# The input norm's vector: eight rows transposed once, and multiplied in at the transposed x

## The chip, the cores and the metric

The kernel runs on one core of a Trainium2 chip. The metric is the device time of one execution in microseconds (us); lower is better. Five engines run side by side, each through its own list of instructions in order: PE (TensorE, the matmuls; its weight loads are listed apart as PEld), DVE (VectorE), ACT (ScalarE), POOL (GpSimd) and SP (SyncE, which here issues DMAs). They wait for each other by semaphores.

## The reference, cut to what matters

One decoder layer on 512 tokens of width 1024, all in float32. It begins with a norm, whose result feeds every projection of the first half:

```python
def rms_norm(x, g):
    xf = x.astype(jnp.float32)
    y = xf * lax.rsqrt(jnp.mean(xf * xf, axis=-1, keepdims=True) + EPS)
    return (y * g.astype(jnp.float32)).astype(x.dtype)

u = rms_norm(x, norm_mix_g[l])
proj = u @ w_in[l]          # q, k, v, the convolution's input, two gates
```

After it come sliding-window attention, a convolution, a gated sum with `w_out`, and an MLP with a second norm. The change touches only the first norm, `u`, and the order of the work around it.

## The kernel before, in words

**Precision.** Every float32 matrix is split into a high part (rounded to the matmul's float32r) and a low part (what is left), and a product is three matmuls: high by high, low by high and high by low. So each operand costs a high copy (ACT, usually) and a low subtraction (DVE or POOL).

**The stretch that the change touches.** The first 38 us make `u` transposed, with channels on partitions (`uTh` and `uTl`, high and low), and from it k and v for all tokens. The 512 tokens are four tiles (t = 0 to 3) of 128. For each tile:

- `x_square(t)`: ACT squares x with a running sum (L296) and takes a root (L297); DVE makes the reciprocal root with a Newton step (L150, L127 to L130).
- `x_scale(t)`: one DVE instruction over 128x1024 multiplies x by the root (one number per partition, that is per token) and by `gmix` (L300). `gmix` is the norm's vector copied to all 128 partitions, since here the channels lie along the free dimension; it comes by a DMA of 128 copies of 4 KB, 512 KB.
- `x_trans(t)`, that is `transpose_split`: for each half of the channels four PE transposes (L207) fill one bank of PSUM, `tp`, a 128x512 tile. Then one ACT copy of 128x512 makes the high part (L209), and one DVE subtraction of 128x512 the low part (L210).
- `k_proj(t)` and `v_proj(t)`, by `tok_proj`: 16 matmuls of 256 columns in eight pairs, for each 128 channels first the high part of u (L316) then the low one (L317) by the weights' high part; then eight by the weights' low part (L320).

The weights of k come in two halves of 512 KB into `kw_raw` (L235), those of v into `vw_raw`. ACT casts each half to its high part (L307); the low parts (L308) are made by POOL for k's first half and by DVE for the other three.

**What sets the order.** From L1341 on this stretch stands in an order written out by hand under `manual_schedule`: each of PE, DVE, ACT and POOL gets its instructions in the order of the calls, and an instruction that waits holds back what stands behind it on its engine. DMAs are issued by SP in program order: x's first tile, `gmix`, the two halves of k's weights, x's second tile, the halves of v's weights, x's last two tiles, then small vectors. Before its first real work PE runs `WARM` = 20 dummy matmuls of the 128x128 identity by itself (`warm_up`, two instructions each, L225), and `FILL` = 4 more between the first tile's transposes and its k. After this stretch the rest (events sorted by position) follows: columns of small vectors (L361), then the projections from L498 on.

Buffers of the `pt` tag are three tiles of 128x1024: `gmix` takes one, and the `u_t` tiles the others in turn. The tiles in PSUM with the tag `tr` are two, so the two halves of a `tp` are two banks.

Of the kernel before, what the change touches and what calls it, by code (L numbers as in the profile page):

```python
# [8 lines left out]
F32 = mybir.dt.float32  # L9
F32R = mybir.dt.float32r  # L10
I32 = mybir.dt.int32
AF = mybir.ActivationFunctionType
# [5 lines left out]
P = 128  # L18
S = 512
# [21 lines left out]
WARM = 20  # L41
FILL = 4
# [11 lines left out]
def tile_hybrid_block(  # L54
# [44 lines left out]
    def bc(ap, n):  # L99
        return ap.partition_broadcast(n)  # L100
# [47 lines left out]
    def mean_eps(ss, n, w, tag):  # L148
        ms = sm.tile([P, w], F32, name=f"ms_{tag}", tag=f"ms{w}")
        ve.tensor_scalar(out=ms, in0=ss, scalar1=1.0 / n, scalar2=EPS, op0=ALU.mult, op1=ALU.add)  # L150
        return ms
# [49 lines left out]
    def transpose_split(ps_pool, src, dst_h, dst_l, t, tag, pt="tr"):  # L201

        for half in range(2):
            tp = ps_pool.tile([P, 4, P], F32, name=f"tp_{tag}_{half}", tag=pt)
            for j in range(4):
                k = half * 4 + j
                pe.transpose(tp[:, j, :], src[half][:, j * P:(j + 1) * P], ident)  # L207
            hs = dst_h[:, half * 4:half * 4 + 4, t * P:(t + 1) * P]
            se.copy(hs, tp)  # L209
            ve.tensor_tensor(out=dst_l[:, half * 4:half * 4 + 4, t * P:(t + 1) * P],  # L210
                             in0=tp, in1=hs.bitcast(F32), op=ALU.subtract)
# [27 lines left out]
    gmix = att.tile([P, D], F32, name="gmix", tag="pt", bufs=3)  # L239
    kw_raw = wp.tile([P, KD, 256], F32, name="raw_k", tag="raw", bufs=2)  # L240
    nc.sync.dma_start(gmix, bc(norm_mix_g[0], P))
# [14 lines left out]
    nsink = rb_sink[:, 32:32 + NQ]  # L256
    nc.sync.dma_start(gq, bc(q_norm_g[0], P))
# [41 lines left out]
    def x_scale(t, rs):  # L299
        ve.scalar_tensor_tensor(out=us[t], in0=xt[t], scalar=rs, in1=gmix, op0=ALU.mult, op1=ALU.mult)  # L300

    def x_trans(t):
        transpose_split(ps1, (us[t][:, 0:S], us[t][:, S:D]), uTh, uTl, t, f"u{t}")
# [1037 lines left out]
    with tc.manual_schedule(engines=START_ENGINES):  # L1341
        se.activation(roots[:, 0:1], epsc, AF.Sqrt)
        x_square(0, ss0)
        x_scale(0, rsqrt_root(root[0], mean_eps(ss0, D, 1, "x0"), 1, "x0"))
        lo0 = hi_lo(kw, kw_raw, 0, se.copy, ge)
        lo0()
        load(0)
        x_trans(0)
        warm_up(FILL)
        lo1 = hi_lo(kw, kw_raw, 1, se.copy, ve)  # L1350
        lo1()
# [12 lines left out]
        x_square(3, ss2[:, 1:2])  # L1364
        next(vp)
        rs2 = rsqrt_root(roots[:, 2:4], mean_eps(ss2, D, 2, "x23"), 2, "x23")
        ksum()
        next(vp)
        x_scale(2, rs2[:, 0:1])
# [3 lines left out]
        x_trans(2)  # L1373
        split_hi(0)
# [3 lines left out]
        for _ in vp:  # L1378
            pass
# [54 lines left out]
```

## Time and profile before

| what | value |
|---|---|
| median of 3 runs | 772.23 us (771.13 to 772.3) |
| the profiled execution | 770.88 us, of which its span is 769.1 us |
| PE busy | 759.5 us (99%) |
| DVE busy | 603.8 us (79%) |
| ACT busy | 440.3 us (57%) |
| POOL busy | 275.2 us (36%) |

The span runs from the first instruction to the end of the last; times in the rows below count from its start. "Busy" is the time in which an engine had an instruction under way. A matmul's record is longer than the interval at which matmuls follow each other, because they are pipelined. A row of the timeline gives start, duration, engine, line of the kernel, operation, output and inputs, sizes (partitions x elements) and count; in square brackets stands the idle time before it and what ended it.

### The profile page before, as it was taken

What the parts mean: (1) busy time and instruction counts of PE and PEld (TensorE: products, weight loads), DVE (VectorE), ACT (ScalarE), POOL (GpSimd) and SP (SyncE); (2) the same over time, 40 slices, a digit from 0 to 9 for tenths busy, and PEclk for the clock granted to TensorE, in tenths of its full rate; (3) what the DMA queues carried; (4) which work ended last, traced back from release to release, by engine and by line L of the source; (5) the groups of instructions that cost most, each with busy time, mean ns of one, the idle gap of its engine ahead of it and who ended that gap; (6) DMA issues with size and microseconds to landing.
All of it is one profiled execution on the core that took longest, in us unless ns stands there. A gap on an engine that the chain in (4) does not pass through costs nothing.

```text
span 769.1 us, 11643 instructions
## 1 busy us (share of the span) xinstructions
PE 759.5 (99%) x4476; PEld 667.8 (87%) x4476; DVE 603.8 (79%) x925; ACT 440.3 (57%) x697; POOL 275.2 (36%) x215
## 2 busy tenths in 40 slices
PE   9999999999999999999999999989999999999997
PEld 8989989897888888888888899868998899889986
DVE  5467978898888888877337678899779987998696
ACT  7445457667667656257325367754675467636761
POOL 1454978958575465524440002210121011101110
PEclk9999999999999999999999999999999999999999
DMA  7441051214132122523318107883588348844772
GB/s 267 151 144 55 1 165 41 98 55 136 56 98 96 55 75 90 192 82 109 105 63 312 69 29 151 205 196 105 145 211 186 116 133 216 178 132 115 167 159 109
DMA packets 65870, 97.48 MB, mean 127 GB/s; under 512 B 3524, under 2 KB 36340, under 8 KB 65814
## 3 DMA queue, kind: packets, MB, share of 16 engines
q1 hardware_dynamic: 56566, 78.91, 31.1%
q0 software_dynamic: 9248, 17.83, 13.7%
q8 instruction: 35, 0.57, 0.3%
q14 instruction: 21, 0.17, 0.1%
HBM read 94.60 MB, written 2.12 MB: 126 GB/s over the span
## 4 chain that ended last, share of the span: by engine, by line
PE 82%; DVE 6%; ACT 3%; DMA 3%; issue 3%; POOL 2%; DVEq 0%; POOLq 0%; ACTq 0%
PE ps_x L1160 9%; PE ps_z L1165 8%; PE ps_y L1160 4%; PE ps_y L1165 4%; DMA block<-in_w_ff_dram 3%; PE ps_x L1165 3%; PE ps_z L1160 2%; PE ps_ta L498 2%; PE ps_ta L500 2%; PE ps_wo L199 2%; PE ps_wo L198 2%; PE ps_wo L197 2%; PE ps_g L498 2%; PE ps_ta L499 2%; PE ps_wc L500 2%
## 5 line engine op out<-in xcount | busy, mean ns | idle before, releaser
L1135 DVE TENSOR_TENSOR piecel<-block,pieceh 128x1024 fp32r<-128x1024 f32 x112 | 136.1, 1222 | 36.2 <-ACT pieceh L1132 36.0
L1132 ACT CAST pieceh<-block 128x1024 fp32r<-128x1024 f32 x112 | 115.9, 1050 | 73.5 <-DVE block L1129 21.4
L1115 POOL DMA_DIRECT2D block<-in_w_ff_dram x34 | 41.3, 1243 | 298.5 <-DVE piecel L1135 174.6
L800 DVE SCALAR_TENSOR_TENSOR cv<-h,wcol,cv 128x512 f32<-128x512 f32 x208 | 147.7, 749 | 0.5
L1160 PE MATMUL ps_x<-xSh,pieceh 128*128 128x256 f32 x192 | 53.9, 281 | 0.4 <-ACT c L1179 0.4
L1160 PE MATMUL ps_x<-xSl,pieceh 128*128 128x256 f32 x192 | 53.9, 281 | 0.0
L1160 PE MATMUL ps_x<-xSh,piecel 128*128 128x256 f32 x192 | 53.8, 280 | 0.0
L709 ACT ACTIVATE s<-s,negm 128x257 f32<-128x257 f32 (+1 forms) x64 | 30.5, 480 | 16.4 <-DVE negm L701 16.4
L1165 PE MATMUL ps_z<-piecel,aSh 128*128 128x512 f32 x96 | 37.9, 395 | 1.7 <-DVE piecel L1135 1.6
L1165 PE MATMUL ps_z<-pieceh,aSh 128*128 128x512 f32 x96 | 37.5, 390 | 0.5 <-ACT pieceh L1132 0.5
L1165 PE MATMUL ps_z<-pieceh,aSl 128*128 128x512 f32 x96 | 37.4, 389 | 0.0
L733 DVE TENSOR_TENSOR pTl<-ptp,pTh 128x512 fp32r<-128x512 f32 x28 | 19.4, 691 | 22.9 <-ACT pTh L729 22.9
L1129 DVE TENSOR_TENSOR block<-block,block 128x1024 f32<-128x1024 f32 x30 | 36.6, 1223 | 0.7 <-DMA block<-in_w_ff_dram 0.3
L1160 PEld LDWEIGHTS ps_x<-xSh,piecel 128*128 128x128 f32 x192 | 36.7, 191 | 0.0
L197 PE MATMUL ps_q<-wh_q,uTh 128*128 128x256 f32 x128 | 36.6, 286 | 0.0
L1160 PEld LDWEIGHTS ps_x<-xSh,pieceh 128*128 128x128 f32 x192 | 36.0, 188 | 0.6 <-ACT c L1179 0.6
L1160 PEld LDWEIGHTS ps_x<-xSl,pieceh 128*128 128x128 f32 x192 | 36.0, 188 | 0.2 <-DVE xSl L1203 0.2
L199 PE MATMUL ps_q<-wh_q,uTl 128*128 128x256 f32 x128 | 36.2, 283 | 0.0
L198 PE MATMUL ps_q<-wl_q,uTh 128*128 128x256 f32 x128 | 36.2, 283 | 0.0
L792 POOL TENSOR_TENSOR side<-side,tap 128x512 f32<-128x512 f32 x24 | 31.1, 1297 | 13.6 <-ACT tap L791 13.6
L1199 ACT CAST aSh<-c 128x1024 fp32r<-128x1024 f32 x16 | 16.8, 1050 | 28.8 <-DVE c L1213 13.2
L718 POOL TENSOR_TENSOR s<-s,r 128x1024 f32<-128x1024 f32 (+1 forms) x16 | 26.9, 1684 | 14.7 <-DVE r L713 14.7
(323 smaller groups left out, 2540.9 us busy)
## 6 DMA issues: line engine op xcount, KB each, us to landing
block<-in_w_ff_dram SPq DMA_DIRECT2D x64, 512.0 KB, 5.0
block<-in_w_ff_dram POOLq DMA_DIRECT2D x34, 512.0 KB, 6.8
x<-in_x_dram SPq DMA_DIRECT2D x8, 512.0 KB, 5.1
raw_g<-in_w_in_dram SPq DMA_DIRECT2D x8, 512.0 KB, 4.5
raw_a<-in_w_in_dram SPq DMA_DIRECT2D x8, 512.0 KB, 3.6
raw_q<-in_w_in_dram SPq DMA_DIRECT2D x8, 512.0 KB, 4.9
raw_ta<-in_w_in_dram SPq DMA_DIRECT2D x8, 512.0 KB, 4.4
raw_tc<-in_w_in_dram SPq DMA_DIRECT2D x8, 512.0 KB, 3.5
```

The source lines that it names most:

```text
L197: pe.matmul(ps, ah, wh, start=first, stop=False)
L198: pe.matmul(ps, ah, wl, start=False, stop=False)
L199: pe.matmul(ps, al, wh, start=False, stop=last)
L498: pe.matmul(ps, wh[:, k, :], ah(k), start=(k == 0), stop=False)
L792: ge.tensor_tensor(out=side[ct], in0=side[ct], in1=tap, op=ALU.add)
L800: ve.scalar_tensor_tensor(out=cps[ct], in0=src, scalar=w, in1=cps[ct], op0=ALU.mult, op1=ALU.add)
L1115: ge.dma_start(tl["raw"][buf][:, ks, :], block(ph, i, j)[:, ks, :], accum_op=ALU.add)
L1129: ve.tensor_tensor(out=o, in0=a, in1=b, op=ALU.add)
L1132: se.copy(tl["ph"][n % 4], tl["raw"][buf][:, 2 * h:2 * h + 2, :])
L1135: ve.tensor_tensor(out=tl["pl"][n % 4], in0=tl["raw"][buf][:, 2 * h:2 * h + 2, :], in1=tl["ph"][n % 4].bitcast(F32), op=ALU.subtract)
L1160: pe.matmul(o, b[:, c, w], a[:, k, :], start=(first and c + q + i == 0), stop=(k == 3 and i == 2), skip_group_check=True)
L1165: pe.matmul(acc, a[:, k, w], b[:, c, :], start=(first and c + i == 0), stop=(k == 3 and i == 2), skip_group_check=True)
```

## The change

The vector comes as eight rows of 128 numbers (`grow`, a DMA of 4 KB) instead of 128 copies of it. One PE transpose into PSUM (`g_ps`) and one DVE copy make of it eight columns, `gcol`: channel on partition, one column for each 128 channels. `x_scale` multiplies by the root alone. `transpose_split` multiplies by the column where it reads the transposed x: for each half, four ACT activations of 128x128 with the column as scale make the high parts, then four DVE instructions of 128x128 (multiply by the column, subtract the high part) the low ones. Where one ACT and one DVE instruction stood there are four of each, for every half of every tile: 32 and 32 in place of 8 and 8.

The written order changes too. `WARM` goes from 20 to 12, `FILL` from 4 to 1, and two dummy matmuls (`WARM2`) come behind the vector's transpose. ACT's cast of the second half of k's weights moves from behind the first tile's transposes to between their two halves. The square of tile 3 and the reciprocal root of tiles 2 and 3 move behind the rest of v for tile 0. The rest of v for tile 1 moves ahead of the next weights' split and of `x_scale(3)`.

```diff
--- before.py
+++ after.py
@@ -38,8 +38,9 @@
 UNIT0 = 42
 END = 152
 RATES = ((16, 1.0), (42, 1.9), (152, 1.35), (1e9, 1.8))
-WARM = 20
-FILL = 4
+WARM = 12
+WARM2 = 2
+FILL = 1
 EARLY = 3
 ENG = mybir.EngineType
 START_ENGINES = {ENG.PE, ENG.DVE, ENG.Activation, ENG.Pool}
@@ -198,17 +199,22 @@
         pe.matmul(ps, ah, wl, start=False, stop=False)
         pe.matmul(ps, al, wh, start=False, stop=last)
 
-    def transpose_split(ps_pool, src, dst_h, dst_l, t, tag, pt="tr"):
+    def transpose_split(ps_pool, src, dst_h, dst_l, t, tag, weight, between, pt="tr"):
 
         for half in range(2):
             tp = ps_pool.tile([P, 4, P], F32, name=f"tp_{tag}_{half}", tag=pt)
             for j in range(4):
                 k = half * 4 + j
                 pe.transpose(tp[:, j, :], src[half][:, j * P:(j + 1) * P], ident)
-            hs = dst_h[:, half * 4:half * 4 + 4, t * P:(t + 1) * P]
-            se.copy(hs, tp)
-            ve.tensor_tensor(out=dst_l[:, half * 4:half * 4 + 4, t * P:(t + 1) * P],
-                             in0=tp, in1=hs.bitcast(F32), op=ALU.subtract)
+            parts = [(tp[:, j, :], weight[:, half * 4 + j:half * 4 + j + 1],
+                      *(d[:, half * 4 + j, t * P:(t + 1) * P] for d in (dst_h, dst_l))) for j in range(4)]
+            for part, w, hs, ls in parts:
+                se.activation(hs, part, AF.Identity, scale=w)
+            for part, w, hs, ls in parts:
+                ve.scalar_tensor_tensor(out=ls, in0=part, scalar=w, in1=hs.bitcast(F32),
+                                        op0=ALU.mult, op1=ALU.subtract)
+            if half == 0:
+                between()
 
     gp = ExitStack()
     gpool = gp.enter_context(tc.tile_pool(name="gpool", bufs=1))
@@ -236,9 +242,9 @@
                           w_in[512 * kh:512 * kh + 512, c0:c0 + 256].rearrange("(k p) c -> p k c", p=P))
 
     xt = [load_x(0)]
-    gmix = att.tile([P, D], F32, name="gmix", tag="pt", bufs=3)
+    grow = att.tile([P, D], F32, name="grow", tag="pt", bufs=3)[0:KD, 0:P]
     kw_raw = wp.tile([P, KD, 256], F32, name="raw_k", tag="raw", bufs=2)
-    nc.sync.dma_start(gmix, bc(norm_mix_g[0], P))
+    nc.sync.dma_start(grow, norm_mix_g[0].rearrange("(k p) -> k p", p=P))
     load_kv(kw_raw, Q_END, 0)
     load_kv(kw_raw, Q_END, 1)
     xt.append(load_x(1))
@@ -254,6 +260,7 @@
     gq = keep.tile([P, HD], F32, name="gq")
     gk = keep.tile([P, HD], F32, name="gk")
     nsink = rb_sink[:, 32:32 + NQ]
+    gcol = rb_sink[:, 48:48 + KD]
     nc.sync.dma_start(gq, bc(q_norm_g[0], P))
     nc.sync.dma_start(gk, bc(k_norm_g[0], P))
     nc.sync.dma_start(nsink, bc(attn_sinks[0], P))
@@ -297,10 +304,10 @@
         se.activation(root[t], ss, AF.Sqrt, scale=1.0 / D, bias=epsc)
 
     def x_scale(t, rs):
-        ve.scalar_tensor_tensor(out=us[t], in0=xt[t], scalar=rs, in1=gmix, op0=ALU.mult, op1=ALU.mult)
-
-    def x_trans(t):
-        transpose_split(ps1, (us[t][:, 0:S], us[t][:, S:D]), uTh, uTl, t, f"u{t}")
+        ve.tensor_scalar(out=us[t], in0=xt[t], scalar1=rs, scalar2=None, op0=ALU.mult)
+
+    def x_trans(t, between=lambda: None):
+        transpose_split(ps1, (us[t][:, 0:S], us[t][:, S:D]), uTh, uTl, t, f"u{t}", gcol, between)
 
     def hi_lo(dst, raw, j, hi_fn, lo_eng):
         ks = slice(4 * j, 4 * j + 4)
@@ -1341,14 +1348,19 @@
     with tc.manual_schedule(engines=START_ENGINES):
         se.activation(roots[:, 0:1], epsc, AF.Sqrt)
         x_square(0, ss0)
-        x_scale(0, rsqrt_root(root[0], mean_eps(ss0, D, 1, "x0"), 1, "x0"))
+        rs0 = rsqrt_root(root[0], mean_eps(ss0, D, 1, "x0"), 1, "x0")
+        g_ps = ps1.tile([P, KD], F32, name="g_ps", tag="tr")
+        pe.transpose(g_ps, grow, ident[0:KD, 0:KD])
+        ve.tensor_copy(gcol, g_ps)
+        warm_up(WARM2)
+        x_scale(0, rs0)
         lo0 = hi_lo(kw, kw_raw, 0, se.copy, ge)
         lo0()
+        lo1 = []
         load(0)
-        x_trans(0)
+        x_trans(0, lambda: lo1.append(hi_lo(kw, kw_raw, 1, se.copy, ve)))
         warm_up(FILL)
-        lo1 = hi_lo(kw, kw_raw, 1, se.copy, ve)
-        lo1()
+        lo1[0]()
         x_square(1, ss1)
         vlo0 = hi_lo(vw, vw_raw, 0, se.copy, ve)
         vlo1 = hi_lo(vw, vw_raw, 1, se.copy, ve)
@@ -1361,22 +1373,22 @@
         vp = v_proj(0)
         next(vp)
         x_trans(1)
-        x_square(3, ss2[:, 1:2])
         next(vp)
-        rs2 = rsqrt_root(roots[:, 2:4], mean_eps(ss2, D, 2, "x23"), 2, "x23")
         ksum()
         next(vp)
+        x_square(3, ss2[:, 1:2])
+        rs2 = rsqrt_root(roots[:, 2:4], mean_eps(ss2, D, 2, "x23"), 2, "x23")
         x_scale(2, rs2[:, 0:1])
         ksum = k_proj(1)
         vp = v_proj(1)
         next(vp)
         x_trans(2)
+        for _ in vp:
+            pass
         split_hi(0)
         split_lo(0)
         x_scale(3, rs2[:, 1:2])
         ksum()
-        for _ in vp:
-            pass
         split_hi(1)
         split_lo(1)
         ksum = k_proj(2)
```

## Rows read from the trace of the kernel before

**Rows 1.** The page, part 1: busy time, share, instructions of each engine.
```profile
PE 759.5 (99%) x4476; PEld 667.8 (87%) x4476; DVE 603.8 (79%) x925; ACT 440.3 (57%) x697; POOL 275.2 (36%) x215
```

**Rows 2.** The chain of waits, in order of time: start, us, what.
```profile
1.47 7.14 PE warm L225 x40
8.61 0.87 PE tp_u L207 x8
...
12.51 0.96 PE ps_k L320 x8
```

**Rows 3.** Timeline of ACT, from 4 us and at 23 us.
```profile
4.13 1.06 ACT L296 ACTIVATE u<-x 128x1024 f32<-128x1024 f32 x1 [1.89 <-DMA x<-in_x_dram]
...
7.84 1.05 ACT L307 CAST kw<-raw_k 128x1024 fp32r<-128x1024 f32 x1 [2.23 <-DMA raw_k<-in_w_in_dram]
9.09 1.07 ACT L209 CAST uTh<-tp_u 128x512 fp32r<-128x512 f32 x2 [0.20 <-PE tp_u L207]
10.05 1.06 ACT L307 CAST kw<-raw_k 128x1024 fp32r<-128x1024 f32 x1
11.00 1.06 ACT L296 ACTIVATE u<-x 128x1024 f32<-128x1024 f32 x1
...
12.39 2.14 ACT L307 CAST vw<-raw_v 128x1024 fp32r<-128x1024 f32 x2
...
23.12 1.08 ACT L209 CAST uTh<-tp_u 128x512 fp32r<-128x512 f32 x2 [1.69 <-PE tp_u L207]
```

**Rows 4.** Timeline of PE and its weight loads, at 13.5, 24.3 and 38 us.
```profile
13.47 0.19 PEld L316 LDWEIGHTS ps_v<-vw,uTh 128*128 128x128 f32 x1 [0.21 <-ACT vw L307]
...
24.30 0.28 PE L316 MATMUL ps_k<-kw,uTh 128*128 128x256 f32 x1
24.48 0.39 PE L317 MATMUL ps_k<-kw,uTl 128*128 128x256 f32 x1
...
38.01 0.50 PE L498 MATMUL ps_g<-uTh,wh_g 128*128 128x512 f32 x1
```

**Rows 5.** Timeline of DVE, 6 to 12 us.
```profile
6.22 0.16 DVE L130 SCALAR_TENSOR_TENSOR roots<-a_x,roots 128x1 f32<-128x1 f32 x1
6.58 1.29 DVE L300 SCALAR_TENSOR_TENSOR u<-x,roots,gmix 128x1024 f32<-128x1024 f32 x1 [0.20 <-DMA gmix<-in_norm_mix_g_dram]
9.71 1.29 DVE L210 TENSOR_TENSOR uTl<-tp_u,uTh 128x512 fp32r<-128x512 f32 x2 [1.84 <-ACT uTh L209]
11.14 1.30 DVE L308 TENSOR_TENSOR kw<-raw_k,kw 128x1024 fp32r<-128x1024 f32 x1
```

**Rows 6.** The dummy matmuls alone, in two stretches: busy (count), granted clock, DMA.
```profile
2.00:6.00 4.00, 4.00 (x21) 4.00 (x20) 1.00 0.90 263
7.00:8.00 1.00, 1.00 (x11) 1.00 (x10) 1.00 1.08 377
```

**Rows 7.** Timeline of ACT, 107 to 112.2 us: instructions with a column as operand.
```profile
107.72 0.39 ACT L709 ACTIVATE s<-s,negm 128x129 f32<-128x129 f32 x1
108.01 0.19 ACT L709 ACTIVATION_READ_ACCUMULATOR s<-s,negm 128x1 f32 x1
...
111.60 0.69 ACT L811 ACTIVATE h<-cv,wcol 128x512 f32<-128x512 f32 x1 [1.64 <-DVE csum L808]
112.19 1.04 ACT L462 CAST wh_g<-raw_g 128x1024 fp32r<-128x1024 f32 x1
```

**Rows 8.** Timeline of DVE: four taps at 65.67 us, a fill at 38 us.
```profile
65.67 2.73 DVE L800 SCALAR_TENSOR_TENSOR cv<-h,wcol,cv 128x512 f32<-128x512 f32 x4
...
38.04 0.38 DVE L364 MEMSET rel<- 16x384 f32 x1
```

**Rows 9.** Timeline, 115.5 to 117 us: four matmuls into one bank and its reader.
```profile
115.70 0.28 PE L694 MATMUL sp<-kTl,qT 128*128 128x256 f32 x1
...
115.94 0.28 PE L694 MATMUL sp<-kTl,qT 128*128 128x256 f32 x1
...
116.26 0.48 DVE L701 CUSTOM_DVE_ANT_0 s<-sp,bias,rb_sink 128x256 f32<-128x256 f32 x1 [0.44 <-PE sp L694]
```

## The prediction, made before the change was run

> **What bounds the kernel now.** The page comes first. PE is busy in 759.5 of 769.1 us [rows 1], so what delays its first dense work delays the end, and what another engine saves counts only where PE waits for that engine. Next the chain of waits: it opens with 40 dummy matmuls, the first tile's transposes (8 in 0.87 us, 0.109 each) and its k (8 in 0.96, so 0.12 for each 256 columns) [rows 2], all on PE. So I take the end to move one for one with the first matmul behind this stretch, `ps_g`.
>
> PE's place in that chain hides who feeds it, so I read the feeders' timelines. ACT casts k's first half at 7.84, after 2.23 us of waiting for its DMA. From 9.09 it runs without a gap: two high parts of u, the cast of k's second half, tile 1's square, two casts for v up to 14.53 [rows 3]. PE's weight load for v waits for that at 13.47 [rows 4]. So in the first tile ACT is the engine that matters. DVE waits 0.20 for `gmix` and ends the scaled x at 7.87 [rows 5], but PE is in its dummies until 8.6 [rows 2], so that wait ends nothing today.
>
> **The first tile, step by step.** I laid each engine's list out in the written order: an instruction starts when the one ahead of it lets it and its operands are there. The same layout of the old list puts v at 13.54 against 13.47 measured, and is 0.2 early at `ps_g`, which comes at 38.01 [rows 4].
>
> *The DMA.* x lands just ahead of 4.13, `gmix` at 6.5, k's first half at 7.8 [rows 3, 5]: 2.4 us of the queue are `gmix`. With 4 KB in its place k's first half lands near 5.5 and ACT casts it at 5.6, when its root is done. Nothing waits for the weights after that. This helps by itself nowhere: u, which the first k matmul needs too, comes later.
>
> *The column.* The root is done at 6.38 as before (6.22 + 0.16 [rows 5]). The list now puts the copy of `gcol` ahead of `x_scale` on DVE, and it needs a transpose that stands behind 24 dummy instructions on PE. In 2.00 to 6.00 the trace shows 21 of them, in 7.00 to 8.00 11 [rows 6]; a record is about two intervals long, so they follow each other every 0.21 us early and every 0.11 late: the slower and the faster level (1.2 and 2.4 GHz), though the granted clock reads 1.00 in both. 24 at the early rate end at 1.47 + 5.2 = 6.7; transpose and copy put `x_scale` at 7.15, 0.57 later than before.
>
> *x_scale* loses its second tensor. Before, 1.29 us [rows 5]. At one element per cycle it would stay; the nearest row without a second tensor is a fill of 384 elements in 0.38 [rows 8], where the 1.1 ns each of the two-tensor rows (below) would make 0.42 for the elements alone. With 0.15 fixed that fill has 0.6 ns each, so 1024 take about 0.75; I take 0.72; bounds 0.72 to 1.28. It ends at 7.9. The transposes start at 7.95, not 8.45 to 8.6, as fewer dummies are in the way.
>
> *High parts on ACT.* No row has 128 columns with a column operand from PSUM, so bounds. One of 129 with a column holds ACT for 0.29 (107.72 to 108.01); one of 512 from PSUM 0.59 (111.60 to 112.19) [rows 7], where the plain ones take 0.48 (two from 9.09 to 10.05) and a plain 1024 takes 0.95 (10.05 to 11.00) [rows 3]. So an element costs 0.92 ns, and 384 fewer leave 0.24. The low end, if only the share of the elements counted, is 0.48 / 4 = 0.12. I take 0.27. Eight of them cost 2.16 us a tile in place of 0.96.
>
> *Low parts on DVE.* One element takes 0.16, 1024 take 1.29 [rows 5], so 1.1 ns each and 0.30 for 128. Taps of 512, which also have a column, are 0.68 apart (2.73 / 4 [rows 8]); 384 fewer leave 0.26. I take 0.33 long and 0.25 apart. Low end, a quarter of one of the two low parts of now, 1.29 / 8 = 0.16. Eight take 2.0 in place of 1.2.
>
> *Do the readers overlap?* The text lets DVE start after the first high part. But four matmuls fill one bank, the reader of the first two results could start after the second (115.70 + 0.28 = 115.98) and starts at 116.26, behind the fourth (115.94 + 0.28), with 0.44 us idle [rows 9]. The program gives a bank to one engine at a time. I expect the same between two readers: DVE starts behind ACT's fourth.
> By the Trainium skill (PSUM — Partial Sum Buffer, section PSUM bank collisions raise a hardware error) two engines must not touch one bank of the same partitions at once, readers included; the row shows it for a write and a read, none for two reads. With it the sum below is +2.0, without it +0.2.
>
> The layout then reads: ACT 8.6 to 9.8 first bank; cast of k's second half to 10.7; second bank 10.6 to 11.8; tile 1's square; casts for v 13.1 to 15.1, where they ended at 14.53. DVE: low parts 9.8 to 10.9 and 11.9 to 12.9, then k's second low weights (1.30 [rows 5]) to 14.14 instead of 12.44. PE's fifth matmul of k's last group (L320) waits for those; v starts at 14.6. So the bound passes from ACT to DVE. **First term: +1.1 us.**
> The Trainium skill (ScalarE: Activation LUTs, section What ACT_TABLE_LOAD costs) gives 186 ns plus 0.833 per element, 93 more per column operand, 93 of overlap: an estimate of 0.29 apart, near the 129-element row. By it the sum is +2.7.
>
> **Tiles 1 to 3.** In tile 2 ACT starts at 23.12 = s [rows 3]; k's first matmul comes at 24.30 (s + 1.18), its second waits 0.06 more than usual for the low part [rows 4]. After: first bank's high parts end at s + 1.18, the second's at s + 2.26, and DVE, confined to the second bank after that, gives the last low part at s + 3.4. PE would need it 15 matmuls after the start, s + 1.18 + 1.8 = s + 2.98. It stalls 0.42 instead of 0.06: **+0.36 each for tiles 2 and 3.** Tile 1, where PE already comes late, adds 0.15.
>
> **Costed at nothing.** `FILL` 4 to 1: PE waits for low parts there either way. `x_square(3)` later: its scaled tile is ready near 22.9, the transposes that read it come at 23.7 in the shifted list, 0.8 spare; without that cover its excess goes straight to PE. The rest of v ahead of the weights' split: PE's order is the same, and the first use of those weights is `ps_g`, over 10 us on [rows 4]. On SP one DMA stands where one stood, ahead of the same DMAs, with 4 KB for 512. POOL's low weights start 2 us earlier and are not late in either list.
>
> **Sum.** 1.1 + 0.15 + 0.36 + 0.36 = +2.0 us. On the profiled execution's 770.88 that is 772.9; the median of the runs shown is 772.23, 1.35 above it, so 774.2.
>
> **The rivals.**
> *Both readers at once.* If DVE may follow ACT part by part, low parts come 0.3 behind high ones, tiles 1 to 3 lose their stalls, and the first tile keeps only the longer ACT stretch: +0.2 (0.5 with 0.30 per part), 772.4. For it: the per-part text. Against: the bank row.
> *Short evacuations are cheap; not slower.* The place is ACT between 8.6 and 15. If a part holds ACT 0.12 and DVE 0.16, the earlier start of the transposes (0.5) and the earlier weights win: -0.85 with banks exclusive, -1.04 without, 771.3. It decides at 0.17 on ACT, where the layout gives -0.1. Against: all ACT rows with a column stay near 0.3. With x_scale or landings better than I allow it could reach -1.6.
> *x_scale stays at 1.28.* Everything in the first tile 0.56 later: +2.75, 775.0. Against: the fill row.
> *The clock.* The dummies now end at 7.3 and PE then waits at 7.3 to 7.9, 9.1 to 10.2 and 11.2 to 12.2, where it was dense from 1.47. Transposes or k at the 0.21 interval would add 0.2 to 0.4, a fall in mid-k up to 1: 774.4 to 775.2. For it: in this trace the rate rises only between 6 and 7 us [rows 6], with PE busy since 1.47.
> *The change does not do what it says* would be a `gcol` copy that waits for a slow small DMA into the same tile (`rb_sink`); tiles here are tracked by part (v's first weight load at 13.47 runs beside ACT's cast of the second half of v's weights into the same tile, to 14.53 [rows 3, 4]), so I give it little.
>
> **How the numbers follow.** Forecast (+1.5 to +3.0) 0.53; both readers at once 0.15; cheap short ones 0.14; x_scale unchanged 0.08; clock 0.08; the rest 0.02. 0.2% (1.5 us) is about what a measurement of this kernel can tell from no change. Of the forecast 0.10 falls inside it, with both-readers 0.15 and 0.05 of the cheap case: same 0.30. Cheap case beyond it: faster 0.09, with 0.01 of the rest 0.10. Slower: 0.43 of the forecast, 0.16 of x_scale and clock, 0.01: 0.60. The range runs from the cheap case's 771.3 to +3.4 (0.30 per part), 775.6; the likeliest's own range is 773.7 to 775.2.
>
> **What would show it.** Right: first DVE low part of each half behind ACT's fourth high part; ACT parts 0.26 to 0.30 apart; x_scale near 0.7 starting near 7.15; v's first matmul near 14.6, its wait put on DVE's `kw`; k's second matmul 0.4 behind its first in tiles 2 and 3; `ps_g` near 40.0. Wrong: low parts interleaved with high ones, parts under 0.2 apart, or `ps_g` at or ahead of 38.

## The result, and the profile after

| kernel | median | range of runs | ratio |
|---|---|---|---|
| before | 771.68 us | 770.7 to 772.58 (6 runs) | |
| after | 774.46 us | 773.78 to 776.43 (6 runs) | 1.0042, 95% interval 1.0031 to 1.0053 |

Slower by 0.42%, some 3.2 us by the ratio and 2.8 by the two medians; 774.2 was forecast. The profiled execution of after is the slowest of its six, 776.43 us with a span of 774.7. `ps_g`, by which the forecast measured the stretch, starts at 40.94 us, 2.93 later than before [rows 4]; near 40.0 was forecast. A second profile of the same kernel (the last experiment) has it at 39.96. Both are used below.

The granted TensorE clock of a whole run (its mean) is 0.999 or 1.00 in some runs of a kernel and 0.992 to 0.998 in others, and the time goes with it: of the 75 runs of the kernel before in three sessions, the 39 at 0.999 or more have a median of 771.03 us, the other 36 one of 772.58. The new kernel's 13 runs of two sessions split into 6 at 773.72 and 7 at 775.98. So at the upper clock the change costs 2.7 us.

The page of after, part 1, answers to [rows 1]:

```profile
PE 761.8 (98%) x4459; PEld 668.7 (86%) x4459; DVE 606.8 (78%) x950; ACT 443.9 (57%) x721; POOL 275.3 (36%) x215
```

PE's busy time rose by 2.3 us with 17 instructions fewer (18 of dummies went, one transpose came): at half clock the same matmuls have longer records. The chain of waits of after (start, us, what) says who holds PE now, where [rows 2] had PE alone:

```profile
8.66 1.14 ACT uTh L212 x4
9.80 0.94 ACT kw L314
10.74 1.05 ACT uTh L212 x4
11.82 0.36 DVE uTl L214
12.22 0.58 PE ps_k L324
...
25.30 1.15 ACT uTh L212 x4
26.48 2.16 DVE uTl L214 x8
28.64 0.33 DVE vv L342
28.97 2.75 DVE u L307
```

High parts on ACT, then low parts on DVE, then PE: the evacuation is on the path in every tile. The last line is a surprise and comes back below.

ACT's timeline of after (start, duration, engine, line, operation, sizes, count, idle before), to be held against [rows 3]:

```profile
7.71 1.04 ACT L314 CAST kw<-raw_k 128x1024 fp32r<-128x1024 f32 x1 [1.91 <-DMA raw_k<-in_w_in_dram]
8.66 1.14 ACT L212 ACTIVATE uTh<-tp_u,rb_sink 128x128 fp32r<-128x128 f32 x4
9.68 1.06 ACT L314 CAST kw<-raw_k 128x1024 fp32r<-128x1024 f32 x1
```

Four parts take 1.02 us to the start of what follows them (8.66 to 9.68), so 0.25 each. The weights' cast waits for its DMA until 7.71, as late as before, and so stands ahead of the first part.

DVE's timeline of after, for [rows 5]:

```profile
6.50 0.16 DVE L1354 COPY rb_sink<-g_ps 128x8 f32<-128x8 f32 x1
6.62 0.75 DVE L307 TENSOR_SCALAR u<-x,roots 128x1024 f32<-128x1024 f32 x1
9.84 1.13 DVE L214 SCALAR_TENSOR_TENSOR uTl<-tp_u,rb_sink,uTh 128x128 fp32r<-128x128 f32 x4 [2.47 <-ACT uTh L212]
11.82 1.13 DVE L214 SCALAR_TENSOR_TENSOR uTl<-tp_u,rb_sink,uTh 128x128 fp32r<-128x128 f32 x4 [0.85 <-ACT uTh L212]
12.86 1.22 DVE L315 TENSOR_TENSOR kw<-raw_k,kw 128x1024 fp32r<-128x1024 f32 x1
```

The first low part starts at 9.84. The fourth high part ends at 8.66 + 1.14 = 9.80: DVE stood idle for 2.47 us although the first high part was done 0.8 us earlier.

PE's timeline of after, for [rows 4]:

```profile
9.08 0.39 PE L323 MATMUL ps_k<-kw,uTh 128*128 128x256 f32 x1 [0.34 <-ACT uTh L212]
10.24 0.39 PE L324 MATMUL ps_k<-kw,uTl 128*128 128x256 f32 x1 [0.78 <-DVE uTl L214]
...
12.22 0.58 PE L324 MATMUL ps_k<-kw,uTl 128*128 128x256 f32 x1 [0.70 <-DVE uTl L214]
12.60 0.42 PE L323 MATMUL ps_k<-kw,uTh 128*128 128x256 f32 x1
...
15.59 0.32 PE L323 MATMUL ps_v<-vw,uTh 128*128 128x256 f32 x1
...
26.49 0.28 PE L323 MATMUL ps_k<-kw,uTh 128*128 128x256 f32 x1
26.88 0.39 PE L324 MATMUL ps_k<-kw,uTl 128*128 128x256 f32 x1
...
40.94 0.50 PE L505 MATMUL ps_g<-uTh,wh_g 128*128 128x512 f32 x1
```

PE waits for a low part twice in tile 0, and 0.39 us between the first two matmuls of k in tile 2 (26.49 to 26.88); tiles 1 and 3 show 0.39 and 0.40. From 12.6 to v's first the matmuls follow each other every 0.21 us (15.59 - 12.60 over 14), where before it was 0.12 [rows 2]. The windows of after (stretch, length, busy and count of PE, PEld, DVE, ACT, POOL, then granted clock, DMA share, GB/s) show why:

```profile
8.50:12.20 3.70, 1.90 (x12) 1.31 (x10) 1.51 (x6) 3.70 (x11) 2.37 (x1) 1.00 1.08 396
12.30:15.50 3.20, 3.20 (x15) 3.20 (x16) 3.06 (x10) 2.69 (x5) 0.00 (x0) 0.50 0.68 249
...
339.90:343.20 3.30, 3.30 (x10) 2.54 (x9) 2.96 (x12) 0.00 (x0) 0.72 (x1) 0.51 0.80 283
```

The granted clock is 0.50, the lower of the two levels (1.2 GHz), through 12.3 to 15.5, behind a stretch in which PE was busy 1.90 of 3.70 us. It fell once more at 340 us, far from the change.

### The profile page after: what moved, and what is told of

Its sections match the earlier page's. It is cut to its first block, busy times and chain, and to the rows that moved or that the text cites. A ratio compares the mean times of both kernels' runs of the same rounds, so it can differ in the third digit from the quotient of the medians.

```text
span 774.7 us, 11660 instructions
## 1 busy us (share of the span) xinstructions
PE 761.8 (98%) x4459; PEld 668.7 (86%) x4459; DVE 606.8 (78%) x950; ACT 443.9 (57%) x721; POOL 275.3 (36%) x215
## 3 DMA queue, kind: packets, MB, share of 16 engines
q0 software_dynamic: 9248, 17.83, 13.5%
## 4 chain that ended last, share of the span: by engine, by line
PE 78%; DVE 8%; ACT 4%; DMA 4%; issue 3%; POOL 2%; SPq 0%; DVEq 0%; ACTq 0%; POOLq 0%
PE ps_x L1167 9%; PE ps_z L1172 8%; PE ps_y L1167 4%; PE ps_y L1172 4%; DMA block<-in_w_ff_dram 3%; PE ps_x L1172 3%; PE ps_z L1167 2%; PE ps_ta L505 2%; PE ps_wo L199 2%; PE ps_wo L200 2%; PE ps_wo L198 2%; PE ps_g L505 2%; PE ps_ta L507 2%; PE ps_ta L506 2%; PE ps_wc L507 2%
```

## The experiments

All are compared with the kernel before on the same chip and in the same rounds. Two marks are read in each profile: the start of v's first matmul (13.48 before) and that of `ps_g` (38.01 before).

| kernel | v | `ps_g` | median us | ratio to before, 95% |
|---|---|---|---|---|
| after | 15.59 | 40.94 | 774.46 | 1.0042 (1.0031 to 1.0053) |
| after, again | 14.65 | 39.96 | 775.79 | 1.0041 (1.0023 to 1.0059) |
| after, PE filled in k | 14.56 | 39.86 | 773.49 | 1.0024 (1.0014 to 1.0034) |
| after, two banks per half | 13.68 | 37.52 | 772.68 | 1.001 (1.0001 to 1.002) |
| after, one wide part per half | 13.32 | 38.06 | 773.35 | 1.0015 (1.0006 to 1.0024) |
| after, k's load first | 14.34 | 39.66 | 776.23 | 1.0054 (1.0033 to 1.0074) |
| two banks, column's copy later | 13.42 | 37.25 | 773.1 | 1.0015 (1.0003 to 1.0026) |
| before, cut in four, no column | 13.64 | 38.29 | 772.94 | 1.001 (0.9997 to 1.0024) |
| before, new order and dummies | 13.62 | 38.08 | 773.6 | 1.0021 (1.001 to 1.0032) |
| before, vector not loaded | 13.80 | 38.17 | 770.96 | one run |
| new norm, old order and dummies | 14.95 | 43.28 | 776.21 | 1.0061 (1.0048 to 1.0074) |
| the same, rest of v first | 14.86 | 40.84 | 774.05 | 1.0035 (1.0023 to 1.0048) |
| the same, tile 3 scaled on ACT | 15.04 | 41.47 | 775.32 | 1.0059 (1.0041 to 1.0076) |

### One bank, one reader

The theory: DVE's low parts stand behind ACT's fourth high part because all four lie in one bank of PSUM. If so, two banks of two parts each let DVE start behind the second.

```diff
-            tp = ps_pool.tile([P, 4, P], F32, name=f"tp_{tag}_{half}", tag=pt)
+            tps = [ps_pool.tile([P, 2, P], F32, name=f"tp_{tag}_{half}a", tag=pt),
+                   aux.tile([P, 2, P], F32, name=f"tp_{tag}_{half}b", tag="aux")]
```

> The changed kernel with each half's transposes in two banks of two parts instead of one bank of four. Theory (a bank has one reader at a time): DVE's first low part starts behind ACT's second high part, 0.5 us earlier than in the changed kernel (9.3 instead of 9.84), the waits of k's second matmul in tiles 2 and 3 fall from 0.40 to 0.12, and without a fall of the clock ps_g comes near 38.4: +0.2 to +0.6 us on the kernel before (up to 1 more with a fall). Rival (DVE waits for all four for another reason, or eight short instructions on ACT alone are the cost): no shift of the first low part, ps_g at 40 or later, +2 us or more.

ACT's and DVE's timelines of this kernel, first half of tile 0:

```profile
8.16 0.63 ACT L212 ACTIVATE uTh<-tp_u_0a,rb_sink 128x128 fp32r<-128x128 f32 x2 [1.18 <-PE tp_u_0a L208]
8.67 0.63 ACT L212 ACTIVATE uTh<-tp_u_0b,rb_sink 128x128 fp32r<-128x128 f32 x2
...
8.82 0.61 DVE L214 SCALAR_TENSOR_TENSOR uTl<-tp_u_0a,rb_sink,uTh 128x128 fp32r<-128x128 f32 x2 [1.19 <-ACT uTh L212]
...
37.52 0.50 PE L505 MATMUL ps_g<-uTh,wh_g 128*128 128x512 f32 x1
```

DVE starts at 8.82, just behind the end of the first bank's second part (8.16 + 0.63 = 8.79), while ACT is in the second bank. With the same instructions and as many of them `ps_g` is 2.4 us earlier than in the second profile of after (39.96), half a microsecond earlier than in the kernel before, and earlier than the theory's 38.4. Up to 0.3 of the 2.4 can be due to k's first half, which landed at 5.91 here and at 7.64 there: the kernel with k's load first, where it landed at 5.89, has `ps_g` at 39.66. The rest, and with it the whole loss of 1.95, goes with the wait for the bank. The edit gives the two parts a tile of their own along with a bank of their own; no run tells the two apart. The rule (PSUM — Partial Sum Buffer, section PSUM bank collisions raise a hardware error, in the Trainium skill: two engines must not be in one bank of the same partitions at once) agrees with the trace: in the 128 banks of `tp` in 14 profiles the first low part starts 0.03 to 0.37 us behind the end of the last high part, never ahead of it.

### Is it the cut or the column?

The kernel before, with its evacuations cut in four but without the column:

```diff
-            se.copy(hs, tp)
-            ve.tensor_tensor(out=dst_l[:, half * 4:half * 4 + 4, t * P:(t + 1) * P],
-                             in0=tp, in1=hs.bitcast(F32), op=ALU.subtract)
+            for part, hs, ls in parts:
+                se.copy(hs, part)
+            for part, hs, ls in parts:
+                ve.tensor_tensor(out=ls, in0=part, in1=hs.bitcast(F32), op=ALU.subtract)
```

> The kernel before (its own norm, order and dummies), with each half's evacuation cut into four copies of 128 on ACT and four subtractions of 128 on DVE, without a column operand. Theory (the column operand and the second arithmetic step carry part of the price, and the bank is given to one reader at a time): a plain copy of 512 from PSUM is 0.48 apart and an element costs 0.92 ns, so 128 plain are 0.13 apart; four make 0.52, ACT's stretch hardly grows, ps_g near 38.1 and the time +0.1 us on the kernel before. Rival (what costs is the number of instructions, column or not): 128 plain are 0.25 apart as the new kernel's are, ps_g near 39.9, +1.9 us. Both expect the first low part of a half behind the fourth high part.

```profile
8.89 1.45 ACT L210 CAST uTh<-tp_u 128x128 fp32r<-128x128 f32 x8
...
9.70 1.68 DVE L212 TENSOR_TENSOR uTl<-tp_u,uTh 128x128 fp32r<-128x128 f32 x8 [1.74 <-ACT uTh L210]
```

Plain parts are 0.157 us apart on ACT (the eight take 1.45: seven steps and the last part's 0.35) and 0.198 on DVE. With the column they are 0.25 and 0.26. So the column (with an activation in place of a plain copy) is 0.092 us of each ACT part, and the column and the second arithmetic step together are 0.06 of each DVE part. Four parts take ACT 0.63 us where one copy took 0.48 [rows 3], and `ps_g` is 0.28 later than before: nearer to the theory's 0.1 than to the rival's 1.9. The low parts again wait for the fourth high part (9.70). The Trainium skill (ScalarE: Activation LUTs, section What ACT_TABLE_LOAD costs) gives 93 ns for each column operand; the 0.092 agrees.

The other side of it, the new kernel with the evacuation in one piece and the first group's column for all four groups (the other three columns of each half are left out):

```diff
-            parts = [(tp[:, j, :], weight[:, half * 4 + j:half * 4 + j + 1],
-                      *(d[:, half * 4 + j, t * P:(t + 1) * P] for d in (dst_h, dst_l))) for j in range(4)]
+            parts = [(tp, weight[:, half * 4:half * 4 + 1],
+                      *(d[:, half * 4:half * 4 + 4, t * P:(t + 1) * P] for d in (dst_h, dst_l)))]
```

> The changed kernel with each half evacuated by one ACT and one DVE instruction of 128x512 again, with one column for all four groups of 128 channels (the other three columns are left out, so u is scaled wrongly). Theory (the short evacuations are the cost): v's first matmul near 13.6, ps_g 38.0 to 38.4, time within 0.6 us of before. Rival (the order, the dummies or the added transpose and copy cost it): ps_g at 39.5 or later, +1.5 us or more.

```profile
8.39 0.69 ACT L212 ACTIVATE uTh<-tp_u,rb_sink 128x512 fp32r<-128x512 f32 x1 [0.60 <-PE tp_u L208]
...
9.11 0.75 DVE L214 SCALAR_TENSOR_TENSOR uTl<-tp_u,rb_sink,uTh 128x512 fp32r<-128x512 f32 x1 [1.47 <-ACT uTh L212]
```

One part of 512 holds ACT for 0.58 (8.39 to the next instruction at 8.97) where four parts held it for 1.02. `ps_g` is at 38.06, that of before. So neither the column nor the cut by itself makes ACT's turn in the bank long; the column paid four times does. The median is 0.15% (1.2 us) up none the less, where 0.6 at most was expected, and this stretch does not explain it: in the profile PE falls behind the kernel before by 1.6 us near 338 us, where the clock falls, and by 1.2 near 480.

### The order and the dummies alone

The kernel before, its own norm, in the new order and with `WARM` 12, `WARM2` 2, `FILL` 1:

```diff
-WARM = 20
-FILL = 4
+WARM = 12
+WARM2 = 2
+FILL = 1
...
-        x_trans(0)
+        x_trans(0, lambda: lo1.append(hi_lo(kw, kw_raw, 1, se.copy, ve)))
```

> The kernel before with its own norm (128 copies of the vector, evacuations of 512), but with the new kernel's order of the list and its fewer dummies (12 + 2 ahead, 1 behind the transposes). Theory (the parts cost, the order and the dummies little): v's first matmul near 13.7, ps_g near 38.4, +0.4 us, granted clock 1.00 through 12.3 to 15.5. Rival (the fewer dummies let the clock fall, whatever the norm): clock near 0.5 for about 3 us between 10 and 16, v's first matmul near 15, ps_g 39.5 to 40, +1.5 to +2.

v's first matmul at 13.62 and `ps_g` at 38.08: the order costs 0.07 us at this mark, and the clock is 1.00 in 12.3 to 15.5. The theory holds for the stretch. Its median is nevertheless 0.21% up; in its profile that comes from 335 to 340 us (1.6 us; the clock is 0.66 there, 1.00 in the profile of the kernel before) and from near 480 us (0.9 us). What makes the second is open.

### The clock

PE's pauses in the first k filled with dummies (8 behind the transposes, 4 in the middle of k):

```diff
-FILL = 1
+FILL = 8
...
+            if t == 0 and name == "k" and k == 3:
+                warm_up(4)
```

> The changed kernel with dummy matmuls where PE waits in the first tile: FILL 1 to 8, and four more between the two halves of k's first pass. Theory (short evacuations, one bank for one reader, cost about 2 us, and PE's waits let the clock fall on top): the granted clock stays 1.00 in 12.3 to 15.5 us, where it was 0.50; v's first matmul comes near 14.7 instead of 15.6; ps_g near 40.0 instead of 40.9; the time stays 1.5 to 2.2 us above the kernel before. Rival (the clock alone makes the change slow): ps_g at 38.0 to 38.5 and a time within 0.5 us of before. Rival (the fall has nothing to do with PE's waits): clock 0.50 there again.

```profile
8.50:12.20 3.70, 3.70 (x34) 3.70 (x33) 1.66 (x7) 3.70 (x11) 2.37 (x1) 1.00 1.07 397
12.30:15.50 3.20, 2.93 (x23) 2.72 (x23) 3.06 (x10) 3.17 (x8) 0.00 (x0) 1.00 0.68 246
```

PE is busy throughout 8.5 to 12.2, the clock stays at 1.00, v comes at 14.56 and `ps_g` at 39.86. But one profile without a fall proves little, as the next shows: the new kernel again, unchanged.

> The new kernel once more, unchanged, for a second profile and more times. Theory (part costs and the bank rule make 1.8 us of the first four tiles, a fall of the clock at 12.3 to 15.5, where there is one, another 1.0): ps_g at 39.8 to 40.0 with a granted clock of 1.00 in 12.3 to 15.5, at 40.9 with 0.50. Rival (the stretch is 2.9 us longer by itself, whatever the clock): ps_g at 40.8 or later with a clock of 1.00. Median 774.3, ratio 1.003 to 1.005.

```profile
12.30:15.50 3.20, 2.93 (x23) 2.73 (x24) 3.06 (x11) 3.17 (x8) 0.00 (x0) 1.00 0.63 227
```

```profile
14.07 0.74 PE L327 MATMUL ps_k<-kw,uTh 128*128 128x256 f32 x4 [0.27 <-DVE ms_x L151]
14.65 0.28 PE L323 MATMUL ps_v<-vw,uTh 128*128 128x256 f32 x1
...
39.96 0.50 PE L505 MATMUL ps_g<-uTh,wh_g 128*128 128x512 f32 x1
```

The same pauses (1.16 us behind k's first matmul, 0.98 in the middle) and no fall. v at 14.65, `ps_g` at 39.96: the theory's 39.8 to 40.0. So the fall, when it comes, costs 15.59 - 14.65 = 0.94 us, and it comes in some runs only. The means of whole runs hint at how often: the profiles with one fall while PE works have a mean of 0.997 or 0.998, the one with two has 0.995. Below 0.997 are 4 of the 13 runs of after and 6 of the 11 of the kernel with k's load first, which has the same pauses; none of the 10 of the filled kernel, none of the 24 of the two kernels with two banks per half, and 1 of 75 of the kernel before. But a mean does not say where a fall stood. In the middle of k it was seen in one profile of 14, and the profile of the kernel with k's load first shows 1.00 there. That the pauses invite the fall is therefore likely, rests on counts alone, and is not shown. The filled kernel's 0.24% beside 0.42% fits that, but `ps_g` in the two profiles without a fall there is nearly the same (39.86, 39.96): filling changes little else.

### The DMA that was to come earlier

The forecast had k's first half land at 5.5; in both profiles of after it landed at 7.6 to 7.7. In the other kernels with the same list of loads it landed at 5.9 to 7.5. So the load of k's first half was put ahead of the eight rows:

```diff
-    nc.sync.dma_start(grow, norm_mix_g[0].rearrange("(k p) -> k p", p=P))
     load_kv(kw_raw, Q_END, 0)
+    nc.sync.dma_start(grow, norm_mix_g[0].rearrange("(k p) -> k p", p=P))
```

> The new kernel with the load of k's first half issued ahead of the load of the eight rows instead of behind it. With one and the same list of loads k's first half has landed at 5.91, 6.26, 6.29, 6.72, 6.76, 7.54 and 7.69 us; with the 512 KB load ahead of it at 7.82, 7.89 and 7.95. Theory (the eight small rows ahead of it in the queue are what makes it late in some runs): it lands by 6.0, its cast on ACT is over before the first high part, ACT's parts start near 8.4 rather than 8.67, ps_g 0.2 to 0.3 earlier in a run without a fall of the clock, 39.6. Rival (its landing scatters with the queue as a whole): it lands anywhere from 6 to 7.7 and ps_g stays at 39.9 to 40.9. By both the time stays within 0.1% of the new kernel's, +0.3 to +0.45% on the kernel before.

```profile
5.91 1.04 ACT L314 CAST kw<-raw_k 128x1024 fp32r<-128x1024 f32 x1
8.30 0.89 ACT L212 ACTIVATE uTh<-tp_u,rb_sink 128x128 fp32r<-128x128 f32 x3 [1.34 <-PE tp_u L208]
```

It landed at 5.89, the cast is over long before the first high part, ACT's parts start at 8.30 instead of 8.66, and `ps_g` is at 39.66, 0.30 earlier than in the second profile of after: by the numbers the theory's side. The median, 0.54% up, is worse all the same: the runs are 773.2 to 774.06 (five at 0.999 or more) or 776.23 to 779.38 (six, whose mean clock is 0.992 to 0.996). One profile can't tell the eight rows' part, or that of the load's own earlier issue (1.18 us instead of 1.60), from the scatter of the landing, 5.9 to 7.7 with one list; that stays open.

The kernel before without any load of the vector (`gmix` filled with ones):

```diff
-    nc.sync.dma_start(gmix, bc(norm_mix_g[0], P))
+    nc.vector.memset(gmix, 1.0)
```

> The kernel before with no load of the vector at all: gmix is filled with ones by a memset on DVE (the vector is left out). Theory (the 512 KB set the landing of k's first half, the prediction's step): it lands at 5.5, half a microsecond after x, and ACT casts it at 5.5 to 5.6. Rival (k's own small packets and the loads behind it set it): 6.3 to 7.7. ps_g in both cases within 0.4 of 38.0.

It landed at 5.91: between the theory's 5.5 and the rival's 6.3 to 7.7. In the three profiles with the 512 KB load ahead of it, it landed at 7.8 to 7.95. So the 512 KB were worth 1.9 to 2.0 us here, and `ps_g` at 38.17 shows that they were worth nothing to the kernel before.

### The old order under the new norm

The new norm with `WARM` 12 + 8, `FILL` 4 and the order of before (the cut shows part of it; the rest of v for tile 1 stands behind the weights' split and `x_scale(3)` again):

```diff
-WARM2 = 2
-FILL = 1
+WARM2 = 8
+FILL = 4
...
+        x_square(3, ss2[:, 1:2])
         next(vp)
+        rs2 = rsqrt_root(roots[:, 2:4], mean_eps(ss2, D, 2, "x23"), 2, "x23")
```

> The change's norm alone (eight rows, one transpose, short evacuations), with the order and the count of dummies of the kernel before (12 ahead of the vector's transpose, 8 behind it, FILL 4). Theory: ps_g 39.4 to 40.0, +1.5 to +2 us on before, and k's second matmul in tiles 2 and 3 late by 0.3 as in the changed kernel. Rival (the new order and fewer dummies are the cost): ps_g near 38.0 to 38.5, within 0.5 us of before.

`ps_g` at 43.28, 3.3 us behind the second profile of after: later than expected. DVE's, POOL's and PE's timelines of this kernel:

```profile
28.58 2.87 DVE L307 TENSOR_SCALAR u<-x,roots 128x1024 f32<-128x1024 f32 x1
...
31.70 0.41 DVE L342 TENSOR_TENSOR vv<-ps_v,vv 128x256 fp32r<-128x256 f32 x1
...
28.52 2.38 POOL L473 TENSOR_TENSOR wl_g<-raw_g,wh_g 128x1024 fp32r<-128x1024 f32 x1 [18.25 <-ACT wh_g L469]
...
32.16 0.39 PE L323 MATMUL ps_v<-vw,uTh 128*128 128x256 f32 x1 [2.10 <-DVE vv L342]
```

The scaling of tile 3, 0.75 us in the other tiles, took 2.87: it began 0.06 us after POOL's pass over 1024 columns and ended 0.55 after POOL's end (28.52 + 2.38 = 30.90). Behind it on DVE stood the low part of v (L342), which frees a bank of PSUM, and PE waited 2.10 us for that. In the kernel before, DVE's scaling began first (DVE's and POOL's timelines):

```profile
24.94 1.28 DVE L300 SCALAR_TENSOR_TENSOR u<-x,roots,gmix 128x1024 f32<-128x1024 f32 x1
...
25.52 2.96 POOL L466 TENSOR_TENSOR wl_g<-raw_g,wh_g 128x1024 fp32r<-128x1024 f32 x1 [14.16 <-ACT wh_g L462]
```

There POOL's pass took 2.96 in place of 2.40, and DVE's its usual 1.28. Whoever comes second waits. Two tests:

```diff
         x_trans(2)
+        for _ in vp:
+            pass
         split_hi(0)
         split_lo(0)
         x_scale(3, rs2[:, 1:2])
         ksum()
-        for _ in vp:
-            pass
```

> The new kernel's norm in the order and with the dummies of the kernel before (which measured ps_g at 43.28 and +0.6%), with one piece of the new order put back: the rest of tile 1's v stands ahead of the split of g's weights and of the third tile's scaling. Theory (the fast x_scale cannot run while POOL's first low split runs, stays 2.87 us on DVE, and the low part of v, which stands behind it, holds PSUM from PE: the 2.38 us stall of PE at 29.8): the low part of v now runs ahead of it, the stall goes, ps_g near 40.9, the time 2.3 us under that kernel's, +0.3% on the kernel before. Rival (the stall comes from the later root of tile 3, or from the bank rule): ps_g stays near 43.3, +0.6%.

```profile
28.48 0.42 DVE L342 TENSOR_TENSOR vv<-ps_v,vv 128x256 fp32r<-128x256 f32 x1
28.81 2.83 DVE L307 TENSOR_SCALAR u<-x,roots 128x1024 f32<-128x1024 f32 x1
```

The scaling is as long as before, but the low part of v stands ahead of it; the stall is gone and `ps_g` is at 40.84, 2.4 us earlier. And with the scaling of tile 3 on ACT:

```diff
+        if t == 3:
+            se.activation(us[t], xt[t], AF.Identity, scale=rs)
+        else:
             ve.tensor_scalar(out=us[t], in0=xt[t], scalar1=rs, scalar2=None, op0=ALU.mult)
```

> The same kernel (new norm, old order and dummies), with the scaling of tile 3 alone on ACT in place of DVE. Theory (DVE's scaling waits for POOL, and ACT's doesn't): ACT takes about 1.1 us for it beside POOL's split, DVE's sum for k and low part of v run 2 us earlier, the 2.38 us stall of PE at 29.8 shrinks under 0.5, ps_g near 41, about 2 us under the kernel whose scaling is on DVE. Rival (any 1024-wide pass over SBUF is slowed while POOL runs): ACT's pass takes 2.5 us or more too, the stall stays over 1.5, ps_g over 42.5.

```profile
28.37 1.21 ACT L308 ACTIVATE u<-x,roots 128x1024 f32<-128x1024 f32 x1
...
28.60 2.40 POOL L476 TENSOR_TENSOR wl_g<-raw_g,wh_g 128x1024 fp32r<-128x1024 f32 x1 [18.40 <-ACT wh_g L472]
```

ACT's pass takes 1.21 beside POOL's, PE's idle time there is 0.21 instead of 2.10, and `ps_g` is at 41.47: near the expectation's numbers, and its rival (any pass over 1024 columns is slow beside POOL) falls. The median moved by less than the mark, 0.59% up against 0.61%; five of its six runs have a mean clock under 0.999, four of the five of the kernel with the scaling on DVE are at 1.00. The Trainium skill (SBUF — State Buffer, section SBUF: two separate sides) says that DVE, in a fast one-tensor mode or with two tensors from SBUF (then only against a GpSimd instruction that reads SBUF), and GpSimd share a pair of ports that the first comer keeps for its whole instruction. The rows here agree: DVE ends 0.55 us behind the end of POOL's pass, and in the kernel before POOL 2.26 behind the end of DVE's (25.52 + 2.96 against 24.94 + 1.28), each somewhat less than what it takes alone. That TENSOR_SCALAR runs in such a mode is inferred from its 0.75 us, against 1.28 with two tensors; no row names the mode.

### A version that might beat both

Two banks per half, and the column's copy behind `x_scale` on DVE:

```diff
-        ve.tensor_copy(gcol, g_ps)
         warm_up(WARM2)
         x_scale(0, rs0)
+        ve.tensor_copy(gcol, g_ps)
```

> The new kernel with each half's transposes in two PSUM banks (as in the run that measured ps_g at 37.52 and +0.1%), and the copy of the column put behind x_scale on DVE, so that x_scale no longer waits for the transpose behind 24 dummy matmuls. Theory (that wait of 0.3 to 0.5 us starts the whole first tile later): x_scale at 6.5, transposes at 7.3, k's first matmul near 8.4, v's near 13.3, ps_g 37.1 to 37.3, the time between 0.1% under and 0.1% over the kernel before. Rival (k's last group waits for DVE's low weights, whose cast on ACT stands where it stood): v's first matmul stays at 13.6 to 13.7, ps_g at 37.5, +0.1%.

```profile
37.25 0.50 PE L505 MATMUL ps_g<-uTh,wh_g 128*128 128x512 f32 x1
```

x_scale starts at 6.54, and the stretch is 0.76 us shorter than before, as the theory had it. The time is not: 0.15% over before. Its profiled run took 771.41 us with no fall of the clock while PE works; eight of its twelve runs have a mean clock under 0.999, and they are at 772.09 to 773.78. In its profile the lead of 0.76 us is 0.37 at 323 us and gone at 484. Whether the lower clock comes more often because of the change or by chance, these runs can't tell. No version beat the kernel before.

## Why the prediction was right, step by step

*The bank.* The step on which the sign hung, that ACT and DVE don't share a bank, held in every tile, and two banks took its whole cost away at `ps_g`. The rival of both readers at once falls.

*The sizes of the parts.* ACT 0.25 apart (0.27 taken; 0.26 to 0.30 was named as the sign, and the estimate of 0.29 was 0.04 too long), DVE 0.26 (0.25), x_scale 0.75 long (0.72, from a fill of 384 columns). The rivals of cheap parts (0.17 or less on ACT) and of an x_scale of 1.28 fall.

*The first tile.* Forecast for v: 14.6; 14.65 without a fall of the clock. That it fits so well is owed in part to two misses of opposite sign. x_scale started at 6.62, not 7.15, since the dummies' faster rate came at 5.5 us and not at 6.5. The transposes so began at 7.43, not 7.95. And k's first half landed at 7.69, not 5.5, so that its cast held ACT until 8.66, the 8.6 of the forecast; where it landed at 5.89 ACT's parts began 0.69 behind the first transpose, which would be 8.12 here.

*DVE as the new bound of k's last group.* In the second profile of after the last four matmuls of k's last group wait until 14.07, when DVE's low weights are done (12.81 + 1.21 = 14.02; the row names the short instruction behind them); that is the step as written. In the first profile the slow clock hides it.

```profile
12.81 1.21 DVE L315 TENSOR_TENSOR kw<-raw_k,kw 128x1024 fp32r<-128x1024 f32 x1
```

*Tiles 1 to 3.* 0.39, 0.40 and 0.40 us between k's first two matmuls; k's pass of tiles 2 and 3 is 0.34 longer than before in each, 0.36 was forecast. Tile 1: k's pass 0.29 longer, the stretch from v's first matmul to its transposes 0.20 shorter, so 0.09 for 0.15.

*The sum.* +1.95 at `ps_g` without the clock's fall, +2.0 forecast. Behind it the profile of the kernel with k's load first, which has no fall of the clock while PE works, goes from +1.65 there to +2.3 at the end: steps of 0.24 near 102 us, 0.34 near 323 and 0.20 near 479, some of it won back later. No experiment took them apart. Two side sums can't be redone from the terms that the prediction gives: 2.0 + 0.56 for an `x_scale` of 1.28 makes 2.6 and not 2.75, and 0.03 more for each of 32 ACT parts makes 3.0 and not 3.4. The forecast does not rest on them.

*The end, and luck.* 774.2 was forecast and 774.46 measured, which is nearer than the change itself: +2.0 against +2.8 by the medians and +3.2 by the ratio. The runs from which the forecast started have a median of 772.23, the six beside the change 771.68; that half microsecond is luck. That the end moves one for one with `ps_g` is only roughly true. In the six profiles with no fall of the clock between `ps_g` and PE's last matmul, a delay of 2.8 to 5.3 us at `ps_g` reaches the last matmul with 0.1 to 0.4 more, the 1.65 of k's load first with 0.7 more, the 0.16 of the vector not loaded not at all, and the lead of 0.76 turns into a lag of 0.5 (one profile each).

*The clock.* The rival that got 0.08 is true beside the forecast, not in its place: a fall of 0.94 us in the middle of k, in some runs. It was weighed as an alternative where it should have stood as an addition with a frequency.

*The 1.35 us* between the profiled execution of before and the median, added as a constant, was no constant: it is most of the distance between runs with and without a fall of the clock; the profiles that show one at 335 to 343 us lose 1.6 there.

*Costed at nothing, rightly but not for the reason given.* The moved square and rest of v were called free. So they nearly are, but the move of v is what keeps the longest new wait off PE (2.4 us at `ps_g` in the old order). After's own rows:

```profile
28.89 2.83 DVE L307 TENSOR_SCALAR u<-x,roots 128x1024 f32<-128x1024 f32 x1
...
28.77 2.41 POOL L473 TENSOR_TENSOR wl_g<-raw_g,wh_g 128x1024 fp32r<-128x1024 f32 x1 [17.55 <-ACT wh_g L469]
```

The scaling, which the chain of waits showed above, ends at 31.72, and the transposes that read it start at 31.79, no later behind v's matmuls than in tile 2. Their first two are 0.16 apart instead of 0.11, and k's first matmul follows their start by 1.87 instead of 1.83: of the 2.1 us of waiting some 0.05 reach PE, and there is nothing to spare. The forecast looked at whether POOL would be late, not at whom POOL would make late.

## What to carry to other kernels

When an evacuation of PSUM is cut into parts for two engines, count the parts by bank: the second engine starts behind the first one's last part in that bank, so a longer turn of the first is paid in full, and two banks give it back. An operation moved to "where the data passes anyway" costs its operand each time it passes, here 0.092 us 32 times on ACT, in place of one operand on an engine with time to spare. And of two passes over SBUF on DVE and POOL the one that starts second can wait for the whole of the other: when a change moves either, look at what runs beside it at its new time, and at what stands behind it on its engine.

## What the hardware showed that I had not expected

K's first half, third in SP's order, landed anywhere from 5.9 to 7.7 us with the same list of loads. The rate of the same dummy matmuls rose from one per 0.21 us to one per 0.11 anywhere from 4.4 us (the filled kernel) over 6.5 (the kernel before) to 7.3 (the same without the vector's load), with PE busy in them since 1.5. The clock fell in the middle of k in one of two profiles of the same kernel, with the same pauses ahead of it. DVE's TENSOR_SCALAR over 1024 columns took 0.75 us alone and 2.83 to 2.87 when POOL's pass had started first.
